# Writing both banks of a two-bank PSUM tile before they are read, and accumulating a quad's seven products in three PSUM tiles

## The chip, the cores and the metric

The kernel runs on one core of one Trainium2 chip. The metric is the device time of one execution in microseconds (us). A core has five engines with a queue each: PE multiplies matrices into PSUM, DVE and ACT do elementwise work and read PSUM, POOL does elementwise work in SBUF, SP issues transfers. PSUM has eight banks of 512 fp32 columns by 128 partitions.

## The reference

Two layers of a transformer block over 512 latent tokens (x) and 256 context tokens, width 1024, batch 1, all in fp32. Each layer runs a SwiGLU half-step, a token-mixing step of three kinds of heads, and a second SwiGLU half-step. In the last layer the context takes no part after the mixing step has read it. What the change touches is the SwiGLU half-step (FFN), four in all:

```python
def swiglu(h, w_in, w_out):
    gate, up = jnp.split(h @ w_in, 2, axis=-1)        # w_in: 1024 x 5632
    return (jax.nn.silu(gate) * up) @ w_out           # w_out: 2816 x 1024

x = x + 0.5 * m(mod_x, 2) * swiglu(modulate(rms_norm(x, g_ffn1), m(mod_x, 0), m(mod_x, 1)), w_ffn1_in, w_ffn1_out)
ctx = ctx + 0.5 * m(mod_c, 2) * swiglu(modulate(rms_norm(ctx, g_ffn1), ...), w_ffn1_in, w_ffn1_out)
```

## The kernel before

Activations are kept transposed, features on partitions and tokens along the free dimension: `xT` (the tile X) holds 8 blocks of 128 features by 768 tokens. To keep fp32 accuracy, every operand of a matmul is split into a high and a low part (`split`: ACT writes the high part, DVE or POOL subtracts it to get the low one), and one product is three matmuls (`mm3`, L404 to L407): high by high, high by low, low by high.

An FFN has 22 blocks of 128 hidden features, taken two at a time (`go`, L870):

- The first pair is a plain block (`plain`, L642): for a token piece (512 latent or 256 context tokens) and a block, 8 `mm3` make the gate in one PSUM bank and 8 make the up part in another; ACT takes the silu of the gate, DVE multiplies, and `split` stores the pair for the down projection. In three of the four FFNs both banks are halves of one two-bank tile `s` (`CFG["PB"]`); in the third they are separate tiles. During the plain block DVE, ACT and POOL also make the sums T of the activations (`t_prep`).
- Each further pair is two quads, one for gate and one for up (`quad`, L746). A quad is a Strassen-Winograd scheme: a 2 x 2 block product (two feature blocks by two token halves t1 and t2) from seven products, each of 4 `mm3`, that is, 12 matmuls of 384 columns (256 in the last FFN, which has latent tokens only). The products are named 1 to 7. Each gets a PSUM tile of its own from a rotation of six buffers (L807), and the outputs are sums of products: ACT copies products 1 and 5 to SBUF (L783, L789), and DVE makes seven additions (L785, L791, L793 and, in `put`, L762). Gate outputs go through silu on ACT; up outputs are multiplied with the gates on DVE (L769) and split, high part on ACT, low part on POOL (L770).
- After the quads of a pair the down projection of the pair before is run (`down`, L813): for each of 8 output blocks m, `mm3` over two (at one place three) hidden blocks, for the 512 latent tokens and then the 256 context tokens, and for each of the two a DVE instruction (L822) that scales the bank and adds it to X. Even m use the two halves of an `s` tile, odd m use two one-bank tiles (`DM`).

PSUM's eight banks: one `g`, two `a`, one `b` (one bank each), and two `s` tiles of two banks. `btile` in the FFN cycles g, a, b, a.

Weights come by DMA into R, and `advance` (L615) issues the next weight's split as soon as enough of the 8 weight slots have been freed; a string (`CFG["ORD"]`) gives the order of products (digits), sums (letters) and calls of `advance` (A) in a quad: `1c6u2eA5dxA37yfAg4hA`. A gate or up weight is first turned into sums by four DVE instructions (L556 to L559) and needs its transfer to have landed. In the first FFN small matmuls of the modulation (`mods`, L274) run beside the quads.

Order: each engine works through its own queue in order. The instructions are placed in these queues at compile time by a list scheduler, which may move an instruction ahead of another of the same engine when no dependence forbids it; semaphores for all dependences through tiles are put in by the framework.

Of the kernel before, what the change touches and what calls it, by code (L numbers as in the profile page):

```python
# [14 lines left out]
AF = mybir.ActivationFunctionType  # L15
ALU = mybir.AluOpType
# [5 lines left out]
NK = 8  # L22
SEQ = 512
# [66 lines left out]
def hybrid_kernel(ctx: ExitStack, tc: tile.TileContext, x, c, ctx_in, c_ctx, w_mod, b_mod, g_ffn1, w_ffn1_in,  # L90
# [3 lines left out]
    nc = tc.nc  # L94
# [20 lines left out]
    reg = {}  # L115
# [27 lines left out]
    def cyc(*fs):  # L143
        n = [0]

        def f():
            n[0] += 1
            return fs[(n[0] - 1) % len(fs)]()
        return f

    ENG = {"P": nc.gpsimd, "V": nc.vector}
# [21 lines left out]
    def stile(name="s"):  # L173
        return pS.tile([128, 1024], F32, name=name, tag="s")
# [26 lines left out]
    r = 0  # L201
# [199 lines left out]
    def w_rows(src, r0):  # L401
        return wload(1024, lambda raw: [(raw, src[r0:r0 + 128, :])])

    def mm3(ps, wh, wl, rh, rl, first, last):  # L404
        nc.tensor.matmul(ps, wh, rh, start=first, stop=False)  # L405
        nc.tensor.matmul(ps, wh, rl, start=False, stop=False)  # L406
        nc.tensor.matmul(ps, wl, rh, start=False, stop=last)  # L407

    def gemm_steps(ps, w, piece):
        t0, t1 = piece  # L410
# [110 lines left out]
    def ffn(l, which, w_i, w_o, pieces, side=None):  # L521
# [120 lines left out]
        def plain(js):  # L642
            ws = []

            def weight(i):
                while len(ws) <= i:
                    ws.append(k8(ready.pop(0)))
                return ws[i]

            def banks(pb):  # L650
                if pb == "s":
                    p_ = stile()
                    return p_, p_[:, 512:1024]
                return [(btile if x == "b" else stile)() for x in pb]

            def part(p_, i, piece, ks):
                w = weight(i)
                p0, p1 = piece
                for k in ks:
                    mm3(p_[:, :p1 - p0], w[0][:, k], w[1][:, k], reg["hH"][:, k, p0:p1], reg["hL"][:, k, p0:p1],  # L660
                        k == 0, k == NK - 1)

            def one(z, j, piece, k0=0, ps=None):
                p0, p1 = piece
                sl = slot(j)
                scnt[0] += 1
                s_ = P[:, 2560 + (scnt[0] % 2) * 512:2560 + (scnt[0] % 2) * 512 + p1 - p0]
                pg, pu = ps or banks(CFG["PB"][0 if side else 1 + which])
                part(pg, 2 * z, piece, range(k0, NK))
                act(s_, pg[:, :p1 - p0], AF.Silu)  # L670
                part(pu, 2 * z + 1, piece, range(k0, NK))
                nc.vector.tensor_tensor(s_, s_, pu[:, :p1 - p0], op=ALU.mult)
                split(sl[:, 0, p0:p1], sl[:, 1, p0:p1], s_, ENG[CFG["PL"][fi]])
                for _ in range((TS1 if side else TS2).pop(0)):
                    next(tgen, None)

            TS1, TS2 = list(CFG["TS1"]), list(CFG["TS2"])
            if side:
                early = [((0, XP), banks("s")), ((0, CP), banks("s")), ((1, XP), (gtile(), btile_()))]
                for (z, piece), ps in early:  # L680
                    for up in range(2):
                        part(ps[up], 2 * z + up, piece, range(4))
                for (z, piece), ps in early:
                    one(z, js[z], piece, 4, ps)
                    if z == 0 and piece is CP:
                        ring[:] = [0, 7]
                        advance(4)
                one(1, js[1], CP)
            else:
                for piece in pieces:  # L690
                    for z, j in enumerate(js):
                        one(z, j, piece)
                        if CFG["AE"] and piece is pieces[-1] and z < len(js) - 1:
                            advance(4)
            for _ in tgen:
                pass
            if side:
                area("W2", 1024, F32)
                advance(3)
            else:  # L700
                advance(4 if CFG["AE"] else 4 * len(js))
# [41 lines left out]

        gates = {}

        def quad(j0, gate):  # L746
            w = []

            def prod(wi, u, rh, rl):
                while len(w) <= wi:  # L750
                    w.append(ready.pop(0))
                wh, wl = w[wi] if wi < 3 else (w[3][:, 0:512], w[3][:, 512:1024])
                ps = bank()
                for k in range(4):
                    o = slice(u * 512 + k * 128, u * 512 + (k + 1) * 128)
                    mm3(ps, wh[:, o], wl[:, o], rh[:, k], rl[:, k], k == 0, k == 3)
                next(beside, None)
                return ps

            def put(z, ts, eng, x, y, r):  # L760

                eng.tensor_tensor(r, x, y, op=ALU.add)  # L762
                i = 2 * z + (ts is t2)
                if gate:
                    act(r, r, AF.Silu)
                    gates[i] = r
                else:
                    sl = slot(j0 + z)
                    ENG[ME[i]].tensor_tensor(r, r, gates[i], op=ALU.mult)  # L769
                    split(sl[:, 0, ts], sl[:, 1, ts], r, ENG[LE[i]])  # L770

            p1, p5, u2, u4 = [tmp() for _ in range(4)]
            ps, freed = {}, [2, 2, 2, 1]
            ops = {
                "1": (0, 0, reg["hH"][:, 0:4, t1], reg["hL"][:, 0:4, t1]), "6": (1, 1, TH[1], TL[1]),
                "2": (0, 1, reg["hH"][:, 4:8, t1], reg["hL"][:, 4:8, t1]), "5": (1, 0, TH[0], TL[0]),
                "3": (2, 0, reg["hH"][:, 4:8, t2], reg["hL"][:, 4:8, t2]), "7": (2, 1, TH[2], TL[2]),
                "4": (3, 0, reg["hH"][:, 0:4, t2], reg["hL"][:, 0:4, t2])}
            for c in CFG["ORD" if j0 > NPL else "ORD1" if gate else "ORD2"]:
                if c in ops:  # L780
                    ps[c] = prod(*ops[c])
                elif c == "c":
                    nc.scalar.activation(p1, ps["1"], AF.Copy)  # L783
                elif c == "u":
                    nc.vector.tensor_tensor(u2, p1, ps["6"], op=ALU.add)  # L785
                elif c == "e":
                    put(0, t1, nc.vector, p1, ps["2"], p1)
                elif c == "d":
                    nc.scalar.activation(p5, ps["5"], AF.Copy)  # L789
                elif c == "x":  # L790
                    ENG[UE[0]].tensor_tensor(u4, u2, p5, op=ALU.add)  # L791
                elif c == "y":
                    nc.vector.tensor_tensor(u2, u2, ps["7"], op=ALU.add)  # L793
                elif c == "f":
                    put(1, t2, ENG[UE[1]], u2, p5, p5)
                elif c == "g":
                    put(0, t2, nc.vector, u4, ps["3"], u4)
                elif c == "h":
                    put(1, t1, nc.vector, u2, ps["4"], u2)
                else:  # L800
                    advance(freed.pop(0))

        btile = cyc(gtile, atile, btile_, atile)

        qb = [0]
# [7 lines left out]
        def down(js, hook=None):  # L813
            ws = [ready.pop(0) for j in js]

            def part(p_, m, piece):
                p0, p1 = piece
                t = 0 if p0 < SEQ else 1
                for a, j in enumerate(js):
                    mm3(p_, ws[a][0][:, m * 128:(m + 1) * 128], ws[a][1][:, m * 128:(m + 1) * 128],  # L820
                        slots[j][:, 0, p0:p1], slots[j][:, 1, p0:p1], a == 0, a == len(js) - 1)
                nc.vector.scalar_tensor_tensor(xT[:, m, p0:p1], p_, dmod[l][:, 3 + which, m, t:t + 1],  # L822
                                               xT[:, m, p0:p1], op0=ALU.mult, op1=ALU.add)

            def body(piece):
                for m in range(NK):
                    part(btile()[:, :piece[1] - piece[0]], m, piece)
                    yield
            if hook is None:
                for m in range(NK):  # L830
                    both = (XP, CP) if CP in pieces else (XP,)
                    if DM[m] == "s":
                        p_ = stile()
                        banks = [p_[:, 0:512], p_[:, 512:1024]]
                    else:
                        banks = [btile() for _ in both]
                    for p_, piece in zip(banks, both):
                        part(p_[:, :piece[1] - piece[0]], m, piece)
                advance(2 * len(js))
            else:  # L840
                hooked(last, body, hook)
# [916 lines left out]
```

## Time and profile before

| | |
|---|---|
| time, median of 3 runs | 3044.97 us (3043.24 to 3045.93) |
| profiled execution | 3044.36 us, its span 3042.6 us |
| PE busy | 2882.5 us (95%), 19464 matmuls |
| DVE busy | 2223.7 us (73%) |
| ACT busy | 1222.9 us (40%) |
| POOL busy | 501.7 us (16%) |
| mean granted PE clock | 0.984 of full speed |

The four FFNs lie at about 50 to 600, 1176 to 1700, 1750 to 2250 and 2680 to 3010 us of the span; between them are the mixing steps. Busy time of PE is modelled: matmuls are pipelined, so the distance between starts is a better measure of one matmul than its length. A row of a list of waits has the waiting engine, the tile it writes and its line, then what released it. A number in brackets at the end of a timeline row is the idle time of the engine before the instruction, and what ended it.

### The profile page before, as it was taken

The page shows a single profiled execution, that of the slowest core. Times are in us where ns is not written, and L with a number is a line of the kernel's source. Part 1 is how long each engine was busy: PE and PEld are TensorE (multiplying, and loading weights), DVE is VectorE, ACT ScalarE, POOL GpSimd, SP SyncE. Part 2 cuts the span into 40 slices and gives each one's busy share as a digit, 9 for nine tenths or more (in the row PEclk, how much of TensorE's full clock was granted, in tenths as well). Part 3 has the DMA queues.
Part 4 walks back from the last instruction along what each step waited for, and adds up shares of the span by engine and source line. Part 5 has one row for each costly group of instructions (what it writes and reads, how often), then busy time and mean ns, then how long its engine had stood idle before and what let it go on. Part 6 is the DMA issues. An engine that isn't in the chain of part 4 may idle for free. (4 is left out here: it accounts for less than half of the span.)

```text
span 3042.6 us, 48615 instructions
## 1 busy us (share of the span) xinstructions
PE 2882.5 (95%) x19464; PEld 2505.7 (82%) x19464; DVE 2223.7 (73%) x3881; ACT 1222.9 (40%) x2310; POOL 501.7 (16%) x484
## 2 busy tenths in 40 slices
PE   6999999999999888999999989999999999889998
PEld 4788889988776567989999889999888866679998
DVE  6767677655668877777776687776664679799996
ACT  4332323344455435323323533323253556354443
POOL 3001010110002433011010311010110012233432
PEclk8999999999999999999999999999999999999999
DMA  6332212313435341212222112122222333223332
GB/s 214 111 118 83 88 58 64 90 40 92 107 107 178 105 125 29 83 57 70 64 62 70 56 56 70 60 65 72 61 70 70 82 110 122 74 70 105 104 98 91
DMA packets 314246, 262.38 MB, mean 86 GB/s; under 512 B 27529, under 2 KB 290341, under 8 KB 314021
## 3 DMA queue, kind: packets, MB, share of 16 engines
q1 hardware_dynamic: 311712, 255.47, 27.8%
q10 hardware_dynamic: 2308, 3.82, 0.4%
q8 instruction: 153, 2.51, 0.3%
q14 instruction: 73, 0.59, 0.1%
HBM read 247.72 MB, written 2.10 MB: 82 GB/s over the span
## 5 line engine op out<-in xcount | busy, mean ns | idle before, releaser
L369 ACT ACTIVATE W0r<-R 128x1024 fp32r<-128x1024 f32 (+2 forms) x229 | 219.7, 965 | 384.7 <-PE a L407 84.6
L370 DVE TENSOR_TENSOR W0r<-R,W0r 128x1024 fp32r<-128x1024 f32 (+1 forms) x193 | 216.1, 1124 | 58.2 <-ACT W0r L369 29.8
L822 DVE SCALAR_TENSOR_TENSOR X<-s,dmod,X 128x512 f32<-128x512 f32 x252 | 158.9, 630 | 134.5 <-PE s L407 134.1
L369 ACT ACTIVATE W1r<-R 128x1024 fp32r<-128x1024 f32 (+1 forms) x149 | 141.7, 952 | 270.9 <-PE a L406 87.6
L370 POOL TENSOR_TENSOR FAr<-P,FAr 128x384 fp32r<-128x384 f32 (+2 forms) x68 | 80.8, 1192 | 597.8 <-ACT FAr L369 563.1
L370 POOL TENSOR_TENSOR FBr<-P,FBr 128x384 fp32r<-128x384 f32 (+1 forms) x60 | 70.5, 1177 | 549.4 <-ACT FBr L369 442.2
L163 ACT ACTIVATE P<-s,sm 128x768 f32<-128x768 f32 (+3 forms) x160 | 119.0, 750 | 59.1 <-DVE sm L1053 36.7
L405 PE MATMUL g<-Hr,W0r 128*128 128x384 f32 (+3 forms) x384 | 135.8, 354 | 1.6 <-ACT P L163 1.5
L406 PE MATMUL g<-Hr,W0r 128*128 128x384 f32 (+3 forms) x384 | 132.0, 344 | 0.0
L370 DVE TENSOR_TENSOR W1r<-R,W1r 128x1024 fp32r<-128x1024 f32 (+1 forms) x102 | 110.2, 1087 | 24.7 <-ACT W1r L369 11.4
L822 DVE SCALAR_TENSOR_TENSOR X<-a,dmod,X 128x256 f32<-128x256 f32 (+1 forms) x170 | 101.8, 599 | 23.3 <-PE a L407 22.9
L556 DVE TENSOR_TENSOR P<-R 128x512 f32<-128x512 f32 x80 | 58.9, 736 | 75.2 <-DMA R<-in_w_ffn_in_dram 75.2
L407 PE MATMUL g<-Hr,W0r 128*128 128x512 f32 (+3 forms) x308 | 108.2, 351 | 1.4 <-DVE W0r L370 1.4
L405 PE MATMUL s<-Hr,W0r 128*128 128x256 f32 (+2 forms) x272 | 91.2, 335 | 12.1 <-ACT P L163 7.1
L407 PE MATMUL a<-Hr,W0r 128*128 128x384 f32 (+2 forms) x308 | 100.0, 325 | 0.0
L1053 DVE TENSOR_REDUCE sm<-s 128x1 f32<-128x768 f32 (+1 forms) x80 | 65.8, 844 | 41.2 <-PE s L1052 41.1
L405 PE MATMUL s<-Hr,W1r 128*128 128x256 f32 (+2 forms) x240 | 78.1, 325 | 15.5 <-ACT P L163 12.8
L406 PE MATMUL s<-Hr,W0r 128*128 128x256 f32 (+2 forms) x272 | 89.7, 330 | 2.5 <-POOL Hr L370 1.7
L407 PE MATMUL s<-Hr,W0r 128*128 128x384 f32 (+2 forms) x264 | 86.5, 328 | 0.0
L370 POOL TENSOR_TENSOR Hr<-P,Hr 128x256 fp32r<-128x256 f32 (+1 forms) x64 | 55.6, 871 | 185.3 <-ACT Hr L369 185.0
L405 PE MATMUL a<-Hr,W0r 128*128 128x384 f32 (+2 forms) x256 | 84.7, 331 | 1.2 <-DVE ms L330 1.2
L405 PE MATMUL b<-Hr,W0r 128*128 128x256 f32 (+3 forms) x256 | 85.1, 333 | 0.8 <-ACT FAf L905 0.4
(855 smaller groups left out, 10210.6 us busy)
## 6 DMA issues: line engine op xcount, KB each, us to landing
R<-in_w_ffn_in_dram SPq DMA_DIRECT2D x164, 512.0 KB, 4.0
R<-in_w_mod_dram SPq DMA_DIRECT2D x104, 512.0 KB, 3.9
R<-in_w_ffn_out_dram SPq DMA_DIRECT2D x40, 1024.0 KB, 4.9
R<-in_w_in_dram SPq DMA_DIRECT2D x28, 512.0 KB, 3.9
W2f<-in_w_mod_dram SPq DMA_DIRECT2D x24, 512.0 KB, 3.5
R<-in_w_ffn_in_dram SPq DMA_DIRECT2D x6, 1024.0 KB, 5.9
Gr<-Bf SPq DMA_DIRECT2D x48, 96.0 KB, 2.2
Hf<-in_w_mod_dram SPq DMA_DIRECT2D x4, 1024.0 KB, 12.4
```

The lines of the kernel that those rows point to most:

```text
L163: i = nc.scalar.activation(dst, src, func, **kw).ins
L369: nc.scalar.activation(dst_hi, src, AF.Copy)
L370: (lo_eng or nc.vector).tensor_tensor(dst_lo, src, dst_hi.bitcast(F32), op=ALU.subtract)
L405: nc.tensor.matmul(ps, wh, rh, start=first, stop=False)
L406: nc.tensor.matmul(ps, wh, rl, start=False, stop=False)
L407: nc.tensor.matmul(ps, wl, rh, start=False, stop=last)
L556: ENG[se[0]].tensor_tensor(SB[:, 0:512], a21, a22, op=ALU.add)
L822: nc.vector.scalar_tensor_tensor(xT[:, m, p0:p1], p_, dmod[l][:, 3 + which, m, t:t + 1], xT[:, m, p0:p1], op0=ALU.mult, op1=ALU.add)
L1053: nc.vector.tensor_reduce(sm[:, s:s + 1], S[:, k0:TOK], AX.X, ALU.max, negate=True)
```

## The change

In `plain`, the matmuls of the up part are issued ahead of the silu that reads the gate. In `down`, `part` is cut in two: the matmuls of both token pieces of a block are issued first (`part`), and then both DVE instructions (`update`). In `quad`, all but the first pair (72 quads) take a new path: one `s` tile and two one-bank tiles are taken at the start, and products are accumulated onto each other by PE. Product order is 1, 2, A, 6, 5, A, 7, 3, A, 4, A. Product 6 goes onto 1 once ACT has copied 1; 7 onto 6 (with 1) once ACT has copied that sum; 3 onto 5 once ACT has copied 5; 4 onto 7's sum once DVE has added it to the copy of 5. ACT makes three copies instead of two, DVE three additions instead of seven, and the last output is read from PSUM by silu or by the multiplication.

```diff
-    def mm3(ps, wh, wl, rh, rl, first, last):
+    def mm3(ps, wh, wl, rh, rl, first, last, onto=False):
+        nc.tensor.matmul(ps, wh, rh, start=first, stop=False, skip_group_check=onto)
+        (the other two likewise)
@@ plain
                 part(pg, 2 * z, piece, range(k0, NK))
+                part(pu, 2 * z + 1, piece, range(k0, NK))
                 act(s_, pg[:, :p1 - p0], AF.Silu)
-                part(pu, 2 * z + 1, piece, range(k0, NK))
@@ quad
+        def quad_onto(j0, gate):
+            w = []
+            pa_, pc_, pb_ = stile()[:, :h], btile()[:, :h], btile()[:, :h]
+            def prod(wi, u, rh, rl, ps, first=True):
+                ...
+                for k in range(4):
+                    o = slice(u * 512 + k * 128, u * 512 + (k + 1) * 128)
+                    mm3(ps, wh[:, o], wl[:, o], rh[:, k], rl[:, k], first and k == 0, k == 3, not first)
+                next(beside, None)
+            def put(z, ts, r, x):
+                i = 2 * z + (ts is t2)
+                if gate:
+                    act(r, x, AF.Silu)
+                    gates[i] = r
+                else:
+                    sl = slot(j0 + z)
+                    (nc.vector if x is not r else ENG[ME[i]]).tensor_tensor(r, x, gates[i], op=ALU.mult)
+                    split(sl[:, 0, ts], sl[:, 1, ts], r, ENG[LE[i]])
+            def add(r, x):
+                nc.vector.tensor_tensor(r, r, x, op=ALU.add)
+            p1, p5, u2, c21 = [tmp() for _ in range(4)]
+            freed = [2, 2, 2, 1]
+            prod(0, 0, hH[:, 0:4, t1], hL[:, 0:4, t1], pa_)
+            nc.scalar.activation(p1, pa_, AF.Copy)
+            prod(0, 1, hH[:, 4:8, t1], hL[:, 4:8, t1], pb_)
+            add(p1, pb_)
+            put(0, t1, p1, p1)
+            advance(freed.pop(0))
+            prod(1, 1, TH[1], TL[1], pa_, False)
+            nc.scalar.activation(u2, pa_, AF.Copy)
+            prod(1, 0, TH[0], TL[0], pc_)
+            nc.scalar.activation(p5, pc_, AF.Copy)
+            advance(freed.pop(0))
+            prod(2, 1, TH[2], TL[2], pa_, False)
+            add(p5, pa_)
+            put(1, t2, p5, p5)
+            prod(2, 0, hH[:, 4:8, t2], hL[:, 4:8, t2], pc_, False)
+            add(u2, pc_)
+            put(0, t2, u2, u2)
+            advance(freed.pop(0))
+            prod(3, 0, hH[:, 0:4, t2], hL[:, 0:4, t2], pa_, False)
+            put(1, t1, c21, pa_)
+            advance(freed.pop(0))
+        def quad(j0, gate):
+            (quad_onto if j0 > NPL else quad_apart)(j0, gate)
@@ down
-                    for p_, piece in zip(banks, both):
-                        part(p_[:, :piece[1] - piece[0]], m, piece)
+                    work = [(p_[:, :piece[1] - piece[0]], m, piece) for p_, piece in zip(banks, both)]
+                    for w in work:
+                        part(*w)
+                    for w in work:
+                        update(*w)
```

## Rows read from the trace of the kernel before

**Rows 1.** The page's line of busy time by engine.
```profile
PE 2882.5 (95%) x19464; PEld 2505.7 (82%) x19464; DVE 2223.7 (73%) x3881; ACT 1222.9 (40%) x2310; POOL 501.7 (16%) x484
```
**Rows 2.** PE's waits, whole span: who, for what; us in total, times, longest.
```profile
PE s L405 <- DVE X L822: 36.9, 43, 3.7
PE s L405 <- ACT P L163: 20.0, 10, 7.1
```
**Rows 3.** PE's waits in 100 to 600, 1150 to 1700 and 1700 to 2250 us.
```profile
PE s L405 <- DVE X L822: 18.4, 8, 3.7
...
PE s L405 <- DVE X L822: 9.7, 16, 1.4
...
PE s L405 <- DVE X L822: 7.8, 15, 1.2
```
**Rows 4.** Timeline, second FFN, down projection: start us, us, engine, line, operation.
```profile
1441.29 0.40 PE L405 MATMUL s<-FAr,W1r 128*128 128x512 f32 x1
...
1441.78 0.74 DVE L822 SCALAR_TENSOR_TENSOR X<-s,dmod,X 128x512 f32<-128x512 f32 x1
...
1442.57 0.39 PE L405 MATMUL s<-FAr,W1r 128*128 128x256 f32 x1 [0.89 <-DVE X L822]
1442.80 0.28 PE L406 MATMUL s<-FAr,W1r 128*128 128x256 f32 x1
1442.91 0.28 PE L407 MATMUL s<-FAr,W2r 128*128 128x256 f32 x1
...
1443.62 0.40 PE L407 MATMUL s<-FAr,W2r 128*128 128x512 f32 x1
1443.86 0.40 PE L405 MATMUL s<-FAr,W0r 128*128 128x512 f32 x1
```
**Rows 5.** Timeline, PE, first matmuls of two products of an up quad.
```profile
1423.11 0.34 PE L405 MATMUL a<-Hr,W2r 128*128 128x384 f32 x1
...
1425.21 0.34 PE L405 MATMUL g<-Gr,W0r 128*128 128x384 f32 x1
```
**Rows 6.** Windows: us, busy time by engine, granted PE clock, DMA share, GB/s.
```profile
239.00:245.00 6.00, 5.47 (x22) 4.60 (x23) 2.76 (x5) 0.37 (x1) 1.01 (x1) 0.72 0.00 0
...
498.00:504.00 6.00, 5.06 (x19) 4.23 (x20) 3.17 (x6) 0.52 (x1) 1.03 (x1) 0.72 0.00 0
```
**Rows 7.** Windows, plain blocks; columns PE, PEld, DVE, ACT, POOL, clock, DMA, GB/s.
```profile
50.00:100.00 50.00, 41.02 (x223) 34.98 (x222) 47.02 (x78) 23.35 (x43) 14.09 (x11) 0.90 0.17 53
1186.00:1216.00 30.00, 21.35 (x128) 18.33 (x127) 29.17 (x41) 12.68 (x24) 13.39 (x11) 0.89 0.00 1
```
**Rows 8.** Timeline row of a copy on ACT; group of such copies (busy us, mean ns).
```profile
1425.41 0.49 ACT L783 ACTIVATE P<-a 128x384 f32<-128x384 f32 x1 [0.16 <-PE a L407]
...
L783 ACT ACTIVATE P<-a 128x384 f32<-128x384 f32 x18 | 8.8, 489 | 8.4 <-PE a L407 8.4
```
**Rows 9.** Timeline, DVE, same up quad; then L556's group in 1218 to 1700 us.
```profile
1428.53 0.69 DVE L556 TENSOR_TENSOR P<-R 128x512 f32<-128x512 f32 x1 [4.00 <-DMA R<-in_w_ffn_in_dram]
1429.14 0.55 DVE L785 TENSOR_TENSOR P<-P,g 128x384 f32<-128x384 f32 x1
1429.60 0.69 DVE L557 TENSOR_TENSOR P<-P,R 128x512 f32<-128x512 f32 x1
...
1430.81 1.22 DVE L370 TENSOR_TENSOR W2r<-R,W1r 128x1024 fp32r<-128x1024 f32 x1
...
L556 DVE TENSOR_TENSOR P<-R 128x512 f32<-128x512 f32 x18 | 13.8, 767 | 32.0 <-DMA R<-in_w_ffn_in_dram 32.0
```
**Rows 10.** Timeline, PE, last FFN: first matmuls of two products of a quad.
```profile
2813.74 0.28 PE L405 MATMUL b<-Hr,W1r 128*128 128x256 f32 x1
...
2815.16 0.28 PE L405 MATMUL a<-A2r,W2r 128*128 128x256 f32 x1
```
**Rows 11.** Window over the quads of the last FFN; columns as in rows 7.
```profile
2710.00:3010.00 300.00, 297.67 (x2089) 274.09 (x2088) 272.77 (x373) 133.42 (x214) 106.75 (x83) 1.00 0.34 104
```
**Rows 12.** ACT's waits in 1218 to 1700 us.
```profile
ACT FBr L369 <- DVE P L769: 33.6, 14, 5.0
```

More of the change, by code (lines that the diff above doesn't have):

```diff
@@ L402, in w_rows @@
         return wload(1024, lambda raw: [(raw, src[r0:r0 + 128, :])])
-    def mm3(ps, wh, wl, rh, rl, first, last):
-        nc.tensor.matmul(ps, wh, rh, start=first, stop=False)
-        nc.tensor.matmul(ps, wh, rl, start=False, stop=False)
-        nc.tensor.matmul(ps, wl, rh, start=False, stop=last)
+    def mm3(ps, wh, wl, rh, rl, first, last, onto=False):
+        nc.tensor.matmul(ps, wh, rh, start=first, stop=False, skip_group_check=onto)
+        nc.tensor.matmul(ps, wh, rl, start=False, stop=False, skip_group_check=onto)
+        nc.tensor.matmul(ps, wl, rh, start=False, stop=last, skip_group_check=onto)
     def gemm_steps(ps, w, piece):
@@ L744, in ffn, with quad_apart @@
         gates = {}
-        def quad(j0, gate):
+        def quad_apart(j0, gate):
             w = []
@@ L801, in quad @@
                     advance(freed.pop(0))
+        def quad_onto(j0, gate):
+            w = []
+            pa_, pc_, pb_ = stile()[:, :h], btile()[:, :h], btile()[:, :h]
+            def prod(wi, u, rh, rl, ps, first=True):
+                while len(w) <= wi:
+                    w.append(ready.pop(0))
+                wh, wl = w[wi] if wi < 3 else (w[3][:, 0:512], w[3][:, 512:1024])
+                for k in range(4):
[15 more added lines that the diff above has]
+            freed = [2, 2, 2, 1]
+            hH, hL = reg["hH"], reg["hL"]
+            prod(0, 0, hH[:, 0:4, t1], hL[:, 0:4, t1], pa_)
[21 more added lines that the diff above has]
+            (quad_onto if j0 > NPL else quad_apart)(j0, gate)
         btile = cyc(gtile, atile, btile_, atile)
@@ L817, in part @@
                 p0, p1 = piece
-                t = 0 if p0 < SEQ else 1
                 for a, j in enumerate(js):
@@ L821, in part, with update @@
                         slots[j][:, 0, p0:p1], slots[j][:, 1, p0:p1], a == 0, a == len(js) - 1)
+            def update(p_, m, piece):
+                p0, p1 = piece
+                t = 0 if p0 < SEQ else 1
                 nc.vector.scalar_tensor_tensor(xT[:, m, p0:p1], p_, dmod[l][:, 3 + which, m, t:t + 1],
@@ L826, in body @@
                 for m in range(NK):
-                    part(btile()[:, :piece[1] - piece[0]], m, piece)
+                    p_ = btile()[:, :piece[1] - piece[0]]
+                    part(p_, m, piece)
+                    update(p_, m, piece)
                     yield
```

## The prediction

> **What bounds the kernel now.** I read the engines' shares first: PE is busy 2882.5 us of 3042.6, DVE 2223.7, ACT far less [rows 1]. PE is the bound, so a change pays only where PE stands idle or runs slowly, and costs only where it makes PE wait. The second view is the list of PE's waits. Two lines lead it, and both are the places that this change reorders: 43 waits, 36.9 us together, of matmuls into a two-bank tile `s` for the residual update of L822, and 20.0 us for an ACT read, which in the FFN is the silu of a plain block [rows 2]. The third view is the same list by stage: the first FFN has few and long waits for L822 (8, up to 3.7 us), the second and third many short ones (16 and 15), which leaves 4 of the 43 elsewhere [rows 3]; the last FFN has no context tokens and writes one bank of its `s` tiles.
>
> That these are waits across banks shows in order of time [rows 4]: DVE reads the 512 columns of one `s` bank from 1441.78 for 0.74 us, and the matmul into the 256 columns of an `s` tile starts at 1442.57, when that read is over. PE meanwhile had issued only one matmul of other work. A product of a quad, by contrast, follows the last one without a gap: product starts lie 2.10 us apart [rows 5], and no quad instruction is among the large waits. So the quads have nothing to give; the down projections and plain blocks have.
>
> **1. Down projections (write both banks, then read).** The wait goes for good in three FFNs: 18.4 + 9.7 + 7.8 = 35.9 us in 39 waits [rows 3]. What is late next: an `s` tile is needed again four output blocks later, since two alternate with the one-bank tiles. A block is six matmuls of 512 columns at 0.24 us and six of 256 at 0.11 (spacing of starts in [rows 4]), 2.1 us, so DVE may lag 8.4 us, more than twice the longest wait. Nothing comes in its place. The read of the first bank may now start one piece (0.7 us) later; that room hides it.
> Two additions. A listed wait is counted from the modelled end of the matmul before. In [rows 4] the start before lies 1.28 us earlier where 0.24 is usual: 1.04 us lost for 0.89 listed. So 39 x 0.15 = 6 us more. And after five of the first FFN's eight waits, which are 2.3 us long on the mean, the granted clock is down to 0.72 over 6 us, that is, part of them at 1.2 instead of 2.4 GHz: 0.28 x 6.0 = 1.7 us in the first and the last of the five [rows 6], 8.5 us together. Sum: 36 + 6 + 8.5 = 50 us.
>
> **2. Plain blocks (up written before the silu reads gate).** Up to 20.0 us of waits [rows 2], and some 5 us of half clock after the three long ones, if each costs what those above cost. But DVE is full exactly here: 47.0 of 50 us in the first FFN, 29.2 of 30 in the second [rows 7]. It makes the sums T and the split weights that the first quad waits for, so PE arrives earlier at a quad that isn't ready. Bounds 0 and 25 us; I take a third, 8 us, as nearest to those full rows.
>
> **3. Quads (72 of them take the new path).** Removed on DVE: seven additions become three, four times about 0.5 us, 2 us a quad and 0.14 ms in all; worth nothing by itself, since DVE isn't the bound. Added on ACT: one copy of 0.49 us [rows 8], on an engine 40% busy: nothing. Kept: 84 matmuls. Moved: the first weight slot comes free a product earlier, and with it a split and SP's load behind it; harmless.
> What is added is four waits of PE on its own accumulator: product 6 for the copy of 1, 7 for the copy of 6, 3 for the copy of 5, 4 for DVE's addition of 7. Between each pair lies one product, 2.1 us. The old code had six buffers in turn and some five products of room. A copy starts 0.1 to 0.2 us after its product and takes 0.49 [rows 8], so 1.4 us of room are left; an addition takes 0.55 (L785 in [rows 9]), about the same room. In a gate quad I find nothing that fills it.
> In an up quad there is something. DVE stands still 4.0 us for weights, until 1428.53, 5.4 us after the quad's start at 1423.11 [rows 5, 9]; the second FFN has eight such waits, 32.0 us. Behind it now stands the addition of product 2, then the multiplication, then ACT's high copy, and on ACT behind that the copy of 6, which product 7 waits for. In the old order all this was off PE's path. Worked out from starts in [rows 9]: 5.4 + 0.6 (L556) + 0.5 (addition) + 0.6 (L557) + 0.5 (multiplication) + 0.5 (high copy, ACT) + 0.5 (copy of 6) + 0.2 for two handovers = 8.8 us, where product 5 ends at 4 x 2.1 = 8.4. So 0.4 us of waiting in each of 27 up quads, 11 us. In the last FFN a product is 1.42 us [rows 10] and DVE 91% busy, 272.8 of 300 us [rows 11]: 1.42 less 0.4 for the work leaves 1 us, and one split of 1.2 us in front eats it. I take 0.5 us for each of its 18 quads, 9 us. Together 20 us. Bounds: 0 if every copy comes as [rows 8] shows; above, two more DVE steps in front (0.6 as L557 and a split of 1.2 us, [rows 9]) make it 2.2 us in each of 36 up quads, 79 us. I take 20, nearest to the row with its 5.4 us.
>
> A rule of the Trainium skill bears on part 1. The page "PSUM — Partial Sum Buffer" (PSUM bank collisions raise a hardware error) holds that two engines must be kept apart in one bank, while accesses to different banks run clean. By that alone the second bank's matmul need not have waited at all, and part 1 would be worth 0 instead of 50 us. The trace differs: the program's semaphores make the wait across banks, 36.9 us of it.
>
> **Sum.** -50 - 8 + 20 = -38 us on the profiled execution's own 3044.4 us (span 3042.6) gives 3006; the median of the runs shown is 0.6 us above it, so I say 3007.
>
> **Rivals.**
> A. The accumulators cost nothing: 3045 - 58 = 2987. For it: ACT's copies come at once in [rows 8], and DVE loses 2 us of work a quad. Against it: the 4 us standstill is there in each up quad.
> B. Slower: ACT's queue turns the DMA wait into a PE wait. ACT already waits 33.6 us in 14 waits, 2.4 us each, for L769, the multiplication of the up quads, with a high copy at its head [rows 12]. If the copy of 6 always comes behind it, and two more DVE steps stand in front, the 79 us of part 3 outweigh the 58: 3066, more if the clock falls after waits of 2.2 us. It decides from 0.8 us in each of 72 quads (58 / 72). Against it: in the old order the copy of product 1 was ahead of such waits, and the additions stand early in the program.
> C. The change doesn't remove the wait: PE waits for a bank to be reused, not for its neighbour. Then parts 1 and 2 give nothing and part 3 costs 20: 3065. Against it is [rows 4], where the read just ended is of a 512-column bank and the write goes to the 256-column one; a bank's own reuse comes four blocks later, and no wait is longer than 3.7 us.
>
> **How the numbers follow.** Forecast 0.51 (its own range 2992 to 3028: plain 0 to 20 us, quads 5 to 40), A 0.23, B 0.18, C 0.08. No change means within 6 us, 0.2%, about what a measurement of this kernel can tell. Forecast and A are faster but for a few per cent at the upper edge: 0.71 faster; 0.08 the same, from there and from the mild end of B; 0.21 slower. The range, 2978 to 3053, leaves out the bad half of B and C and the tail below A.
>
> **What would show it.** After: PE's waits for the residual update nearly gone in the first three FFNs; granted clock near 1.00 there; the waits for silu partly replaced by waits for splits or T; PE waits of 0.3 to 0.6 us in up quads for the copy of product 6, few in gate quads. I am wrong on part 3 if PE's waits in quads sum to under 5 or over 45 us, on part 1 if any L822 line above 8 us is left.

## The result, and the profile after

The changed kernel takes 3007.7 us (median, 3003.8 to 3010.7) where the kernel before takes 3045.4 on the same chip: ratio 0.988, 95% interval 0.986 to 0.989. The forecast was 3007. The profiled execution took 3008.2 us, its span is 3006.3, against 3044.4 and 3042.6 before. The sum was right, in part by luck: one of the three terms under it was near for the reason given, the second isn't shown at its size, and the third came near its size for the wrong reasons.

Line numbers move by one (L405 to L406, L556 to L557), the residual update from L822 to L885. In the new quads L839 copies product 1, L845 the sum 1+6, L847 product 5; L833 makes the three additions, L829 the multiplications.

Busy time by engine, the page of the kernel after (compare [rows 1]): VectorE has 288 instructions fewer (4 in each of 72 quads) and 146 us less work, ScalarE 72 copies more.
```profile
PE 2863.7 (95%) x19464; PEld 2503.8 (83%) x19464; DVE 2077.4 (69%) x3593; ACT 1252.0 (42%) x2382; POOL 512.1 (17%) x484
```
PE's waits over the whole span, kernel after (us in total, times, longest; compare [rows 2]). No line for L885 is left. The silu's 20.0 us on tile `s` are gone, but one wait for it on tile `g` has grown from 1.5 to 9.8 us, and the waits for L673 (a plain block's multiplication) and L451 (the normalisation) from 1.1 and 1.2 to 7.9 and 4.2 us. The two lines of L833 are new. The three small lines before, then the kernel after:
```profile
PE g L405 <- ACT P L163: 1.5, 1, 1.5
PE s L405 <- DVE P L450: 1.2, 1, 1.2
PE s L405 <- DVE P L672: 1.1, 1, 1.1
```
```profile
PE g L406 <- ACT P L163: 9.8, 1, 9.8
PE s L406 <- DVE P L833: 9.5, 8, 1.6
PE s L406 <- DVE P L673: 7.9, 3, 6.2
...
PE s L406 <- DVE KLf L833: 4.6, 2, 3.1
PE s L406 <- DVE P L451: 4.2, 1, 4.2
```
Windows of the first FFN, kernel after (columns as in [rows 7]). The first two lie at the times of [rows 6], where the program is 7 to 28 us further on by now; the third takes in the whole stretch of the eight waits. The granted clock is 1.00 in all three, against 0.72 in [rows 6].
```profile
239.00:245.00 6.00, 6.00 (x36) 5.26 (x35) 2.54 (x5) 0.07 (x1) 0.00 (x0) 1.00 0.00 0
...
498.00:504.00 6.00, 6.00 (x36) 6.00 (x35) 2.47 (x3) 3.38 (x6) 0.00 (x0) 1.00 0.24 61
...
100.00:560.00 460.00, 456.64 (x2691) 419.78 (x2690) 302.06 (x445) 156.70 (x237) 43.16 (x36) 1.00 0.30 92
```
Timeline of a down projection in the second FFN, kernel after, the place of [rows 4]: the matmuls of 256 columns follow those of 512 into the same `s` tile at the usual spacing, 0.24 us, and VectorE reads the two banks one after the other, when both are written (x2 at 1404.64).
```profile
1402.54 0.40 PE L407 MATMUL s<-FAr,W0r 128*128 128x512 f32 x1
1402.77 0.39 PE L408 MATMUL s<-FAr,W0r 128*128 128x512 f32 x1
1403.01 0.28 PE L406 MATMUL s<-FAr,W1r 128*128 128x256 f32 x1
1403.12 0.28 PE L407 MATMUL s<-FAr,W1r 128*128 128x256 f32 x1
...
1404.64 1.13 DVE L885 SCALAR_TENSOR_TENSOR X<-s,dmod,X 128x512 f32<-128x512 f32 x2
```

To find where the time went I compare the start of the same matmul (counted from the first) in the two traces. The changed kernel is 31.0 us ahead when the second FFN starts, 47.9 at its end, 55.6 near the end of the third, 56.8 at the start of the last FFN, and only 36.2 at the end. So three FFNs gain and the last one gives back 20.6 us. It shows in the waits of the last 316 us, kernel after:
```profile
PE s L406 <- DVE P L833: 9.0, 6, 1.6
PE s L406 <- DVE KLf L833: 4.6, 2, 3.1
```
PE there waits 13.6 us in eight waits for an addition, just ahead of product 4: in seven of the nine up quads and in one gate quad. Counted by the spacing of starts these eight cost 14.9 us. One of them, kernel after, in order of time (bracket: idle before, and what ended it):
```profile
2768.11 0.74 DVE L557 TENSOR_TENSOR P<-R 128x512 f32<-128x512 f32 x1 [1.07 <-DMA R<-in_w_ffn_in_dram]
2768.88 0.69 DVE L558 TENSOR_TENSOR P<-P,R 128x512 f32<-128x512 f32 x1
...
2768.98 1.74 POOL L559 TENSOR_TENSOR R<-R 128x512 f32<-128x512 f32 x1 [0.68 <-DVE P L557]
...
2769.49 2.31 DVE L370 TENSOR_TENSOR W2r<-R,W1r 128x1024 fp32r<-128x1024 f32 x1
2771.73 0.41 DVE L833 TENSOR_TENSOR P<-P,s 128x256 f32<-128x256 f32 x1
...
2772.19 0.38 PE L406 MATMUL s<-Hr,W0r 128*128 128x256 f32 x1 [1.52 <-DVE P L833]
```
VectorE makes two sums and a split for later weights, 3.6 us without a break, and only then the addition that PE's own accumulator waits for. The split takes 2.31 us beside GpSimd's sum, where it takes 1.22 alone [rows 9]. Splits of 2.26 to 2.27 us stand beside that sum in the last FFN of the kernel before too, but there no wait of PE for an addition is listed.

And an up quad of the second FFN, kernel after, where I had put the loss (compare [rows 9]). VectorE stands 4.83 us for weights, as foreseen, with the addition of product 2 behind it. But ScalarE makes the copy of 1+6 (L845) at 1389.24, ahead of the high copy (L369) that hangs on VectorE.
```profile
1387.81 0.69 DVE L557 TENSOR_TENSOR P<-R 128x512 f32<-128x512 f32 x1 [4.83 <-DMA R<-in_w_ffn_in_dram]
1388.42 0.55 DVE L833 TENSOR_TENSOR P<-P,b 128x384 f32<-128x384 f32 x1
...
1389.24 0.49 ACT L845 ACTIVATE P<-s 128x384 f32<-128x384 f32 x1 [1.09 <-PE s L408]
1390.02 0.55 DVE L829 TENSOR_TENSOR P<-P 128x384 f32<-128x384 f32 x1
...
1390.61 0.53 ACT L369 ACTIVATE FBr<-P 128x384 fp32r<-128x384 f32 x1 [0.87 <-DVE P L829]
```
So product 7 has its bank in time. The copy stands ahead of the high copy in all 18 up quads of the second and third FFNs. In the nine of the first FFN it stands behind, as I had expected, but there VectorE waits only 8.1 us for weights, in five waits, and over the whole span one weight load of PE waits 0.2 us for a copy of 1+6. In the second and third FFNs together, PE's waits for an addition are:
```profile
PE s L406 <- DVE P L833: 0.5, 2, 0.3
```

### The profile page after: what moved, and what is told of

It is laid out like the page before. It is cut to its first block, busy times and chain, and to the rows that moved or that the text cites. A ratio compares the mean times of both kernels' runs of the same rounds, so it can differ in the third digit from the quotient of the medians.

```text
span 3006.3 us, 48228 instructions
## 1 busy us (share of the span) xinstructions
PE 2863.7 (95%) x19464; PEld 2503.8 (83%) x19464; DVE 2077.4 (69%) x3593; ACT 1252.0 (42%) x2382; POOL 512.1 (17%) x484
## 4 chain that ended last, share of the span: by engine, by line
PE 82%; DVE 10%; ACT 2%; DMA 2%; issue 2%; POOL 1%; SPq 0%; ACTq 0%; DVEq 0%; POOLq 0%
PE s L406 10%; PE s L408 10%; PE s L407 10%; PE a L406 7%; PE a L407 7%; PE a L408 7%; PE g L406 3%; PE g L408 3%; PE g L407 3%; PE b L406 3%; PE b L408 3%; PE b L407 3%; PE b L274 1%; DVE Hf L1487 1%; PE a L1296 1%
## 5 line engine op out<-in xcount | busy, mean ns | idle before, releaser
L369 ACT ACTIVATE W0r<-R 128x1024 fp32r<-128x1024 f32 (+2 forms) x229 | 219.9, 965 | 342.4 <-PE b L407 154.9
L369 ACT ACTIVATE W1r<-R 128x1024 fp32r<-128x1024 f32 (+1 forms) x149 | 141.7, 952 | 225.5 <-PE b L407 132.4
L885 DVE SCALAR_TENSOR_TENSOR X<-s,dmod,X 128x512 f32<-128x512 f32 x252 | 149.9, 629 | 115.6 <-PE s L408 115.6
L406 PE MATMUL s<-Hr,W0r 128*128 128x384 f32 (+2 forms) x428 | 140.1, 327 | 13.9 <-ACT Hr L461 4.8
L885 DVE SCALAR_TENSOR_TENSOR X<-a,dmod,X 128x512 f32<-128x512 f32 (+1 forms) x170 | 115.1, 677 | 49.3 <-PE a L408 48.9
L557 DVE TENSOR_TENSOR P<-R 128x512 f32<-128x512 f32 x80 | 71.3, 892 | 101.9 <-DMA R<-in_w_ffn_in_dram 101.9
L370 DVE TENSOR_TENSOR W1r<-R,W1r 128x1024 fp32r<-128x1024 f32 (+1 forms) x102 | 113.1, 1115 | 39.6 <-ACT W1r L369 13.0
L407 PE MATMUL s<-Hr,W0r 128*128 128x384 f32 (+2 forms) x428 | 138.6, 324 | 1.1 <-DVE Hr L462 0.8
L408 PE MATMUL s<-Hr,W0r 128*128 128x384 f32 (+2 forms) x408 | 132.1, 324 | 0.0
L406 PE MATMUL s<-Hr,W1r 128*128 128x384 f32 (+2 forms) x324 | 105.8, 327 | 13.7 <-DVE P L673 7.9
L406 PE MATMUL g<-Hr,W0r 128*128 128x512 f32 (+3 forms) x292 | 106.9, 366 | 10.0 <-ACT P L163 9.8
L407 PE MATMUL s<-Hr,W1r 128*128 128x384 f32 (+2 forms) x324 | 104.9, 324 | 0.0
L407 PE MATMUL g<-Hr,W0r 128*128 128x512 f32 (+3 forms) x292 | 103.2, 353 | 0.0
L408 PE MATMUL s<-Hr,W1r 128*128 128x384 f32 (+2 forms) x304 | 99.5, 327 | 0.0
L406 PEld LDWEIGHTS s<-Hr,W0r 128*128 128x128 f32 x428 | 80.6, 188 | 22.1 <-DVE P L833 5.4
L408 PE MATMUL g<-Hr,W0r 128*128 128x512 f32 (+3 forms) x272 | 97.0, 357 | 1.4 <-DVE W0r L370 1.4
```

Of the source, the lines that this page charges most:

```text
L369: nc.scalar.activation(dst_hi, src, AF.Copy)
L370: (lo_eng or nc.vector).tensor_tensor(dst_lo, src, dst_hi.bitcast(F32), op=ALU.subtract)
L406: nc.tensor.matmul(ps, wh, rh, start=first, stop=False, skip_group_check=onto)
L407: nc.tensor.matmul(ps, wh, rl, start=False, stop=False, skip_group_check=onto)
L408: nc.tensor.matmul(ps, wl, rh, start=False, stop=last, skip_group_check=onto)
L557: ENG[se[0]].tensor_tensor(SB[:, 0:512], a21, a22, op=ALU.add)
```

## The experiments

Ratios are to the kernel before on the same chip, with 95% intervals. "Ahead" is the comparison at the same matmul.

**One part at a time.** Three kernels: the kernel before with the diff of `down` alone, of the quads alone, of `plain` alone.
```
e1_down    only  part(...); part(...); update(...); update(...)
e2_quads   only  quad -> quad_onto for j0 > NPL
e3_plain   only  part(pg), part(pu), then act(Silu)
```


> The kernel before with the down projections alone changed (both banks written, then read). Theory: the whole gain of the change is here. PE's lost time before the matmuls of the down projections fell from 74 to 21 us in the first three FFNs between the two traces, so this kernel should take 3045 - 53 = 2992 us, less than the full change (3008), and the L822 waits of PE (36.9 us) should be nearly gone. Rival: a good part of that fall is due to the quads' new path, which takes four additions from DVE in each quad and so lets DVE come to the residual updates sooner; then this kernel gets only about half, 3018 us.

e1 took 2987.8 us, ratio 0.982 (0.980 to 0.984), 55 us less than before. Of PE's 43 waits for the residual update (L825 here) five short ones are left, all in the last FFN, which writes one bank of its `s` tiles:
```profile
PE s L405 <- DVE X L825: 1.1, 5, 0.4
```
The theory holds, a little stronger than forecast.

> The kernel before with the quads alone changed (accumulated in three PSUM tiles). Theory: the path costs nothing in the first three FFNs and some 20 us in the last one, where DVE's addition of product 7 comes late: 3045 + 20 = 3065 us, with about 14 us of PE waits for that addition, nearly all in the last FFN. Rival (DVE relief): with four additions fewer per quad DVE is less late at the down projections too, the L822 waits fall from 36.9 to about 15 us, and the kernel is at 3040 us or below.

e2 took 3023.5 us, 0.993 (0.992 to 0.995): a gain of 20 us, and the rival was right. With the old `down` the cross-bank wait shrinks from 36.9 us in 43 waits to this (PE's waits, e2; its update is L882):
```profile
PE s L406 <- DVE P L833: 8.9, 6, 1.5
...
PE s L406 <- DVE X L882: 5.6, 9, 1.2
```
It is 39.6 us ahead near the end of the third FFN, 38.5 before the last, and gives back 14 us there. So most of the same wait goes from either side: by writing both banks first, or with quads that leave the reader less to do. The two gains don't add: near the end of the third FFN `down` alone is 55.7 us ahead, the quads alone 39.6, both 53.5 (e7).

> The kernel before with the plain blocks alone changed (up part written before the silu reads the gate). Theory: worth 4 us (3041), since DVE is full there and PE then waits for what DVE and ACT deliver next. Rival: the 20 us of waits for the silu are saved in full, with the half clock behind them: 3020 to 3025 us.

e3 took 3047.6 us, 1.001 (1.000 to 1.002): no gain; neither theory. PE's waits in e3 show why: the first row is the first quad's, for a bank whose silu now comes later, the others are waits for VectorE, grown as after the whole change.
```profile
PE g L405 <- ACT P L163: 9.8, 1, 9.8
...
PE s L405 <- DVE P L672: 8.6, 3, 6.2
...
PE s L405 <- DVE P L450: 4.2, 1, 4.2
```
The last FFN lost 5 us, the first three gained 1 to 2.

**The plain part within the change.** The changed kernel with the old `plain`.
```
                 part(pg, 2 * z, piece, range(k0, NK))
+                act(s_, pg[:, :p1 - p0], AF.Silu)
                 part(pu, 2 * z + 1, piece, range(k0, NK))
-                act(s_, pg[:, :p1 - p0], AF.Silu)
```


> The changed kernel without the plain blocks' part. Alone that part measured 1.0012 of the time before: some 2 us gained in the first three FFNs and 5 lost in the last. Theory (it stays a small loss beside the others): 3008 - 3 = 3005 us, within noise of the change. Rival (with DVE relieved by the quads it is now worth its 8 us): 3016 us.

3011.2 us, 0.990 (0.988 to 0.991). Against the changed kernel's 0.988 that is some 6 us for the plain part, but the intervals overlap, and e12 below, which runs as the changed kernel does, has 0.990 too. So no worth of the plain part is shown here.

**Is the last FFN the quads' loss?** The changed kernel with the old quads in the last FFN.
```
-            (quad_onto if j0 > NPL else quad_apart)(j0, gate)
+            (quad_onto if j0 > NPL and fi < 3 else quad_apart)(j0, gate)
```


> The changed kernel, but with the old quads in the last FFN. Theory: the last FFN's loss of 20 us comes from its accumulated quads, 14 us of it listed as waits for the addition of product 7: 3008 - 18 = 2990 us. Rival: the loss there comes from the plain block, which is reordered in that FFN too, or from a start in another state: then only the 13 us of listed waits in later quads or less come back, 2998 to 3005 us.

2989.1 us, 0.982 (0.980 to 0.984), and the theory holds: 17 us of the changed kernel's time are the accumulated quads of the last FFN. The same 250 us of both, after first, then e4 (columns as in [rows 7]): PE is busy 248.6 us instead of 238.4, although VectorE has 40 us more to do. Between the same two matmuls, at its start and in its last quad, the last FFN lasts 332.8 us before, 353.1 after and 337.2 in e4; the eight waits for an addition, 14.9 us, are nearly all of the 15.9 that e4 wins back. The last FFN of e4 still loses 4.3 us, to the plain part, as in e3.
```profile
2710.00:2960.00 250.00, 238.35 (x1631) 218.20 (x1630) 184.42 (x233) 106.37 (x178) 82.30 (x68) 1.00 0.31 92
```
```profile
2710.00:2960.00 250.00, 248.57 (x1749) 229.06 (x1748) 224.76 (x310) 109.59 (x176) 88.28 (x70) 1.00 0.33 100
```

**Is it the wait of product 4 for the addition of 7?** Product 4 gets a bank of its own in the last FFN; a copy and an addition come back.
```
-            prod(3, 0, hH[:, 0:4, t2], hL[:, 0:4, t2], pa_, False)
-            put(1, t1, c21, pa_)
+            if fi == 3:
+                nc.scalar.activation(c21, pa_, AF.Copy)
+                prod(3, 0, hH[:, 0:4, t2], hL[:, 0:4, t2], pb_)
+                add(c21, pb_)
+                put(1, t1, c21, c21)
...
```


> The changed kernel, but in the last FFN product 4 goes to a bank of its own (the one that product 2 has left) instead of onto the bank that DVE's addition of product 7 has to read first; ACT copies the sum with 7, and DVE adds product 4 to it. That takes away one of the four accumulator waits, the one that the trace names in the last FFN, and adds a copy and an addition off PE's path. Theory (this wait is the last FFN's loss): 3008 - 13 = 2995 us, no L833 wait of PE left in the last FFN. Rival (the FFN is short of DVE or ACT time as a whole, or the wait passes to the copies of 1, 6 and 5): 3003 to 3010 us, with new waits in place of the old.

3002.5 us, 0.987 (0.985 to 0.988): by the ratios 3 us better than the change or nothing; the last FFN lasts 348.8 us, 4.3 less than after. The rival holds. The waits for additions are gone (13.6 to 0.2 us), but in the last FFN PE now waits in the down projections for the residual update, L891 in e5:
```profile
PE s L406 <- DVE X L891: 7.9, 11, 0.9
```
VectorE's delay is handed to its next user. The wait of product 4 is where the loss shows; take it away, and most of the loss shows elsewhere.

**Do the slow splits make VectorE late?** The sums of the last FFN that GpSimd makes are put on VectorE.
```
-CFG = dict(... small=('VPVV', 'PPPP', 'VVVV', 'VVPP', 'VV') ...)
+CFG = dict(... small=('VPVV', 'PPPP', 'VVVV', 'VVVV', 'VV') ...)
```


> The changed kernel with the last FFN's weight sums all on DVE (two of the four were on POOL). In its up quads a DVE weight split of usually 1.2 us takes 2.3 us beside a POOL addition, and the addition of product 7 comes behind it. Theory (the slow split makes the addition late, so PE's wait of 1.5 us falls to about 0.5): 3008 - 8 = 3000 us. Rival (it is late because of the standstill for the transfer ahead of it, and two more DVE instructions of 0.6 us make it later): 3008 to 3014 us.

3002.9 us, 0.987 (0.986 to 0.988). One group of splits in the last FFN, after and then e6 (count, busy us, mean ns):
```profile
L370 DVE TENSOR_TENSOR W0r<-P,W0r 128x1024 fp32r<-128x1024 f32 x6 | 10.7, 1789 | 2.3 <-PE a L408 2.3
```
```profile
L370 DVE TENSOR_TENSOR W0r<-P,W0r 128x1024 fp32r<-128x1024 f32 x6 | 7.9, 1310 | 1.1 <-PE a L408 1.1
```
The waits for additions fall from 13.6 to 8.3 us, and the last FFN lasts 348.4 us, 4.7 less than after. The stretched splits are a part of the loss, some 5 us of waits, though VectorE now makes the sum itself (0.7 us) in the same place, so the edit doesn't price them alone. The whole kernel's gain by the ratios, 2 to 3 us, lies within the intervals.

**Does moving the addition forward help?** In the last FFN the second `advance` is issued behind the addition of 7.
```
-            advance(freed.pop(0))
+            if fi < 3:
+                advance(freed.pop(0))
             prod(2, 1, TH[2], TL[2], pa_, False)
             add(p5, pa_)
+            if fi == 3:
+                advance(freed.pop(0))
```


> The changed kernel with one step moved in the quads of the last FFN: the second advance of the weight preparation (whose sums and split VectorE makes) is issued behind the addition of product 7 instead of ahead of it. Theory (product 4 waits for the addition of 7 because two sums and a split of 0.7 to 2.3 us each stand ahead of it in VectorE's queue): the waits for the additions, 13.6 us in the last FFN of the changed kernel, fall under 4 us, and 8 to 15 us of the some 17 that the last FFN's quads cost come back, 2993 to 3000. Rival (VectorE's delay is only handed on, as when product 4 had a bank of its own: splits come later and PE waits for weights, for a residual update or for another addition): the time is 3001 to 3010.

3011.1 us, 0.990 (0.988 to 0.991), no better. The edit did not do what it was meant to. VectorE's queue in e12, the last FFN:
```profile
2801.36 1.07 DVE L557 TENSOR_TENSOR P<-R 128x512 f32<-128x512 f32 x1 [0.75 <-DMA R<-in_w_ffn_in_dram]
2802.46 0.69 DVE L558 TENSOR_TENSOR P<-P,R 128x512 f32<-128x512 f32 x1
2803.07 2.31 DVE L370 TENSOR_TENSOR W0r<-R,W0r 128x1024 fp32r<-128x1024 f32 x1
2805.30 0.41 DVE L833 TENSOR_TENSOR P<-P,s 128x256 f32<-128x256 f32 x1
```
The sums and the split still stand ahead of the addition. More than that: by line, tile and shape, each compute engine runs the same instructions in the same order as in the changed kernel, all 19464 of PE and 3593 of VectorE among them. The program's order changed and the queues' order did not. So e12 says nothing on the theory, and an order with the addition in front wasn't tried; but it tells what a repeat of the changed kernel gives: 3011.1 us and 0.990 where the first gave 3007.7 and 0.988, with a last FFN of 353.5 us against 353.1.

**Why does product 7 not wait in the first three FFNs?** The copy of 1+6 is made by VectorE there.
```
-            nc.scalar.activation(u2, pa_, AF.Copy)
+            (nc.vector.tensor_copy(u2, pa_) if fi < 3 else nc.scalar.activation(u2, pa_, AF.Copy))
```


> The changed kernel with the copy of products 1+6 out of the stile bank made by VectorE instead of ScalarE in the first three FFNs; the quads of the last FFN as they are. Theory (product 7 doesn't wait in the changed kernel only because ScalarE makes that copy ahead of the high copy of the slot, while VectorE stands for a DMA with the addition of product 2 behind it): with the copy in VectorE's queue, behind the standing, product 7 waits for VectorE in the up quads of these FFNs, 0.4 to 1 us in each of 27, and the time is 11 to 27 us more than the changed kernel, 3015 to 3035. Rival (one product's room covers the standing whichever engine copies): no wait for the copy in the list, and the time stays within 5 us of 3008.

3019.0 us, 0.992 (0.990 to 0.993), 11 us more than the changed kernel and 8 more than its repeat e12, at the lower end of the theory's range. Timeline of e10, third FFN: the copy stands behind the wait for weights, and PE waits for it.
```profile
1795.94 0.69 DVE L557 TENSOR_TENSOR P<-R 128x512 f32<-128x512 f32 x1 [6.17 <-DMA R<-in_w_ffn_in_dram]
1796.55 0.55 DVE L833 TENSOR_TENSOR P<-P,b 128x384 f32<-128x384 f32 x1
1797.02 1.22 DVE L370 TENSOR_TENSOR W0r<-R,W0r 128x1024 fp32r<-128x1024 f32 x1
1798.15 0.55 DVE L829 TENSOR_TENSOR P<-P,KLf 128x384 f32<-128x384 f32 x1
1798.62 0.55 DVE L845 COPY P<-s 128x384 f32<-128x384 f32 x1
...
1799.22 0.44 PE L406 MATMUL s<-Ar,W1r 128*128 128x384 f32 x1 [1.20 <-DVE P L845]
```
Thirteen weight loads of product 7 wait 7.5 us for it, and two more 0.9, where one waited 0.2 us for ScalarE's copy; most are shorter than the one shown. The rest of the 8 to 11 us isn't in these waits.

**Is it VectorE's relief that gains in e2?** e2 with four maxima of a tile with itself put back into each quad of the first three FFNs.
```
+            def same(r):
+                if fi < 3:
+                    nc.vector.tensor_tensor(r, r, r, op=ALU.max)
             def add(r, x):
                 nc.vector.tensor_tensor(r, r, x, op=ALU.add)
+                same(r)
...
+            same(p5)
```


> The kernel before with the change to the quads alone, and in the first three FFNs four additions' worth of DVE work put back into every quad: a maximum of a tile with itself, 128x384, in place, after each of the three additions and after the copy of product 5 (the values stay as they are). Theory (the quads alone gained some 20 us because VectorE, rid of four operations a quad, comes to the residual updates in time, so that the cross-bank wait of the down projections shrinks from 36.9 to 5.6 us): the waits for X come back to 25 us or more, the gain of some 40 us by the end of the third FFN falls to 10 us or less, and the time is 3045 to 3065, the last FFN's 15 us of loss included. Rival (the gain comes from the accumulators themselves, fewer banks taken and fewer reads of PSUM, whatever VectorE has to do): the waits for X stay under 10 us, and the time is 3020 to 3030.

3035.2 us, 0.997 (0.996 to 0.998), between the two. The waits for the update (L888 here) come back from 5.6 to 17.3 us:
```profile
PE s L406 <- DVE X L888: 17.3, 25, 1.9
```
Near the end of the third FFN it is 20.8 us ahead instead of 39.6. So putting the work back takes away about half of what the quads gain there; what the other half is stays open. The maxima also stand between an addition and what reads its result, so that load and delay aren't separated.

**The best version.** The changed `down`, quads accumulated in the first three FFNs only, the low parts of the last four tiles' quads on VectorE, `plain` as before (e8); and the same with the changed `plain` in the first three FFNs (e11).
```
-                    split(sl[:, 0, ts], sl[:, 1, ts], r, ENG[LE[i]])
+                    split(sl[:, 0, ts], sl[:, 1, ts], r, ENG["V" if j0 >= NFF - 4 else LE[i]])
```


> What the first four runs point to: down projections changed, quads accumulated in the first three FFNs only, plain blocks as before, and in the last two pairs the low parts of the quads' outputs on DVE instead of POOL (PE waited 8 us for them at the down projection right behind). Theory (each saves what its rows show): the down projections alone gave 2988; the accumulated quads add 2 to 4 us there and the low parts some 4: 2981 us. Rival (quads and down projections remove the same lateness once, nothing adds up): 2986 to 2990 us.

> The version that has been fastest so far (down projections changed; quads accumulated in the first three FFNs only; the low parts of the last four tiles' quads on VectorE; plain blocks as before) with the plain blocks changed too in the first three FFNs, as before in the last. Theory (the plain part is worth some 6 us where the down projections no longer wait): 2973 to 2977. Rival (what the plain part gives is eaten by the same quads' banks as when it was alone): 2979 to 2984.

e8 took 2980.4 us, 0.980 (0.978 to 0.981), e11 2978.2, 0.978 (0.977 to 0.980). Both beat both kernels. e8 is where its theory put it, e11 between its theory and its rival. Their intervals overlap; e8's overlaps that of e1's `down` alone (0.980 to 0.984), e11's ends just below it: the edit of `down` gives most of it. What the low parts on VectorE are worth by themselves wasn't tried.

## Why the prediction was right, step by step

Taken one after the other, `down` alone gives -55 us (e1), the quads on top of it +25 (0.990 of e7 less 0.982 of e1, times 3043), the plain part on top of both -6, and nothing if the repeat e12 is taken for the changed kernel. The forecast had -50, +20 and -8. Each term is off by 2 to 8 us; that the sum came within 1 us is luck.

**Part 1, right.** The wait was across banks, and writing both banks first removes it whole in the three FFNs that write both. To check the size: the spacing of the starts of these FFNs' matmuls, less the usual spacing of their shape, sums to 74 us ahead of matmuls of the down projections before, 21 after, a gain of 53 where I had 36 + 6 + 8.5. By the page "PSUM — Partial Sum Buffer" of the Trainium skill (PSUM bank collisions raise a hardware error) alone, which has accesses to different banks run clean, the part was worth 0; the runs show the wait, 36.9 us of it, and that the order in the program makes it.

**Part 2, its size not shown.** The cover that I named, VectorE full at that place, took the gain: waits of 23.8 us (20.0 and 1.5 for the silu, 1.2 and 1.1 for VectorE) became one of 9.8 at the first quad's bank and 12.1 for VectorE, 21.9 together, and the first two quads of the last FFN wait 4.1 us for an addition (L764) where they waited for none before. I had looked for splits and sums there; the longest is for the bank that the late silu still held. That the part costs 4 to 5 us in the last FFN I had not seen. By the starts of the same matmuls it gains 2 to 5 us up to the end of the third FFN (55.6, and 57.1 in e12, against 53.5 in e7; 67.2 in e11 against 62.1 in e8), and the last FFN takes that back. So in the whole change the part is worth near nothing, not the 8 us that I put down.

**Part 3, a sum that came near by luck from two wrong terms.** The step that failed is "on ACT behind that the copy of 6, which product 7 waits for". I read the program's order as the engine's order. The scheduler may move an instruction ahead where no dependence forbids it, and in the 18 up quads of the second and third FFNs it put the copy ahead of the high copy; in the first FFN it did not, but VectorE hardly stands there. So the 11 us in 27 up quads were nearly nothing: with `down` changed, the kernel with and without the new quads (e7 and e1) stand 53.5 and 55.7 us ahead near the end of the third FFN. e10 shows that the standing itself was read rightly: with the copy behind it PE waits.
The second term, 9 us in the last FFN, was mis-sized. It measured 16 to 17 (e4, and 20.6 us lost there less 4.3 by the plain part). I had one split of 1.2 us in front of one addition, and 0.5 us in each of 18 quads; two sums and a split of 2.31 us stand there, and eight quads wait 1.9 us each by the spacing of starts. The Trainium skill ("SBUF — State Buffer", Who interferes with whom) says that an instruction of VectorE with two inputs in SBUF contends with one of GpSimd that reads SBUF. The trace agrees, 1.22 against 2.31 us, and e6 takes a part of it away. Why VectorE is late for its next user too when product 4 no longer waits (e5 wins back only 4.3 us there) is open. Of the 25 us of e7 over e1, the traces place 16 in the last FFN, 2 in the first three and 3 in the mixing steps between, where nothing was changed.
PE's listed waits for its own accumulator, all for an addition, sum to 14.1 us, inside the 5 to 45 that I had set; that test couldn't tell the two errors from a hit.

**"Worth nothing by itself", wrong.** That holds only once `down` no longer waits for VectorE (53.5 against 55.7 us ahead). Beside the old `down` the quads gain 20 us (e2), and about half of what they gain in three FFNs goes when VectorE gets its work back (e9). An engine that isn't the bound still sets when PE's banks come free.

**Rivals.** A (2987) would have held without the accumulated quads of the last FFN: e4 is at 2989. B did not come, since where VectorE stands long the copy of 6 isn't behind ScalarE's high copy. C is out by e1.

## What to carry to other kernels

Where a tile spans two banks and the framework tracks the whole tile, issue all writes before the first read: a matmul stream otherwise waits for a read of the other bank. Accumulating products onto one another in PSUM saves additions, but ties PE to the engine that reads in between with one product's room. Beside the new `down` it cost 2 us where a product is 2.1 us long, and 16 to 17 where it is 1.42 us and 3.6 us of other work stands in that engine's queue; which of the two decides wasn't tried. Price each part beside the others: two edits that remove the same wait don't add. Read the order of an engine's queue from a trace, not from the program: one copy was moved ahead, and one edit of the order left every queue as it was.

## What the hardware showed beyond that

VectorE's split of 128x1024, 1.22 us alone, took 2.28 to 2.31 us in the seven up quads of the last FFN where it started while GpSimd's sum of 128x512 (L559) ran, and that sum took 1.71 to 1.74 instead of 1.30. It can go the other way: at 2871.86 us a split that started 0.03 us after such a sum (L560) kept its 1.21 us, and the sum took 2.40. The granted clock, 0.72 in the two 6 us windows of [rows 6], is 1.00 from 100 to 560 us of the kernel after, where PE no longer stops for the residual update. The mean over the span says little: 0.984 before, 0.986 after, 0.984 in its repeat e12, 0.989 in e11.
